# A hybrid decoder step on one core: four instead of three prompt blocks through gathered experts, begun early, with their value rows summed on TensorE

## The chip, the cores and the metric

The kernel runs on one core of a Trainium2 chip. Five engines work beside each other, each with its own queue of instructions that it takes in order: TensorE (PE, matmuls), VectorE (DVE), ScalarE (ACT), GpSimd (POOL), and SyncE (SP), which here only starts transfers. The metric is the time of one execution in microseconds (us).

## The reference, cut to what matters

One layer: a projection, an S5 scan with a GLU beside attention over latent keys, an output mix, and then PEER, a retrieval over 16384 one-neuron experts. 1024 prompt tokens (eight blocks of 128) and 32 tokens of short sequences go through it. The part that the change touches is PEER; per token and head the sixteen best of 128 x 128 key pairs are selected, so 128 experts a token:

```python
s1, i1 = lax.top_k(s[:, :, 0], PEER_TOPK)
s2, i2 = lax.top_k(s[:, :, 1], PEER_TOPK)
top, sel = lax.top_k(cand, PEER_TOPK)                  # of the 16 x 16 sums
idx = jnp.take_along_axis(cidx, sel, axis=-1)
g = jax.nn.softmax(top, axis=-1)
act = jax.nn.gelu(jnp.einsum('qhkd,qd->qhk', jnp.take(u_tab, idx, axis=0), xb))
out = jnp.einsum('qhk,qhkd->qd', g * act, jnp.take(v_tab, idx, axis=0))
```

## The kernel before, in words

The stages follow each other: input projection and S5 tables, the S5 scan, GLU and the queries, keys and values (until about 353 us), attention over the prompt blocks, the output mix (`mix_out`), the scores of the keys (`score`), the selection (`select`), the gates (`Gates`), and the experts. The attention of the short rows over their paged cache (`Sample`) stands later in the text, but the scheduler, which lays the instructions out on a simulated clock and fixes the order of each engine, sets much of it beside the prompt's attention.

PEER is done in two ways. Five blocks (`ND`, 640 tokens) are *dense*: `Gates` turns the selected pairs into a table of gate weights over all 16384 experts, written to DRAM (`g_d`), and `Dense` multiplies the tokens with every expert. It takes four second keys at a time (`group`); per second key it loads and splits 128 rows of each table into two parts of reduced precision (`split`: a cast on ACT, a difference on DVE), makes the first product `da` in two halves of 320 tokens (`mm3`, three matmuls a term), applies GELU on ACT and the gates on DVE, splits again, and after four keys makes the second product, `dres` for two blocks that stay in PSUM and `dy` for three whose sums DVE adds into `yac`.

The other three blocks and the short rows are *sparse* (`peer_sparse`): for each of a token's 128 slots POOL gathers one expert row per partition, a tile of 128 x 1024, by an indirect DMA into a ring of five tiles (`RB`). The first table's tiles `pu` are multiplied with the token and summed by DVE (L1328), the second table's tiles `pv` are weighted and added into `pacc` by DVE (L1336). The gathers and both operations stand in the text behind the dense stage and are set beside it. Selection of the sparse blocks is also beside the dense stage.

`weave` sets one list of steps between another by weights that the steps give out.

Of the kernel before, what the change touches and what calls it, by code (L numbers as in the profile page):

```python
# [20 lines left out]
D = 1024  # L21
# [13 lines left out]
class Small:  # L35
    """Elementwise helpers on small fp32 tiles."""
# [107 lines left out]
def rstd_of(nc, pool, ss, n, cols, inv, name, gain=1.0):  # L144
    """gain / sqrt(ss * inv + eps) for [n, cols], with one Newton step."""
# [11 lines left out]
def rstd_dve(nc, pool, ss, n, cols, inv, name, gain=1.0, bufs=None):  # L157
    """gain / sqrt(ss * inv + eps) for [n, cols]: exponent estimate and three Newton steps."""
# [92 lines left out]
def build(ctx, nc, tc, a):  # L251
# [69 lines left out]
    hold = ctx.enter_context(tc.tile_pool(name="hold", bufs=1))  # L321
    idx = hold.tile([128, NSP, 128], I32, name="idx")
    gws = hold.tile([128, NSP, 128], F32, name="gws")
    idn = hold.tile([128, NS], I32, name="idn")
    gwn = hold.tile([128, NS], F32, name="gwn")
    es = ExitStack()
    with right():
        smp = Sample(es, nc, tc, a, ident, keep, x1_d, xn_d)
    dense, sparse = list(range(ND)), list(range(ND, NB))
    wq_d = dram.tile([16, 128, 2, 8, 128], F32R, name="wq_d")  # L330
    drive(attention(nc, tc, a, ident, qkv, o_d, dense + sparse, lambda pool: split_wq(nc, a, pool, wq_d)))
    drive(mix_out(nc, tc, a, ident, gl_d, o_d, x1_d, xn_d, dense + sparse + [NB]))

    xd = ctx.enter_context(tc.tile_pool(name="xd", bufs=1))
    xt = (xd.tile([128, 8, TD], F32R, name="xdh"), xd.tile([128, 8, TD], F32R, name="xdl"))
    er = ExitStack()
    slots = er.enter_context(tc.tile_pool(name="slots", bufs=1))
    i1T = slots.tile([128, TD], F32, name="i1T")
    i2T = slots.tile([128, TD], BF16, name="i2T")
    wT = slots.tile([128, TD], F32, name="wT")  # L340
# [7 lines left out]
    def take_dense(b, i1, i2, w, pool, pp):  # L348
        tp = pp.tile([128, 3, 128], F32, name=f"slt{b}", tag="slt")
        for j, (src, dst) in enumerate(((i1, i1T), (i2, i2T), (w, wT))):  # L350
            nc.tensor.transpose(tp[:, j], src, ident)
            nc.scalar.copy(dst[:, b * 128 : b * 128 + 128], tp[:, j])

    def take_sparse(b, i1, i2, w, pool, pp):
        ns = 128 if b < NB else NS
        f = pool.tile([128, 128], F32, name=f"fi{b}", tag="cand")[:, :ns]
        nc.vector.scalar_tensor_tensor(f, i1, 128.0, i2, OP.mult, OP.add)
        nc.vector.tensor_copy(idx[:, b - ND] if b < NB else idn, f)
        nc.gpsimd.tensor_copy(gws[:, b - ND] if b < NB else gwn, w)

    with ExitStack() as er2:
        tv, ti = tops(er2, ND, "d")
        drive(score(nc, tc, a, ident, xn_d, dense, lambda b: tv[:, b], lambda b: ti[:, b], "d", wq_d, xt))
        pools = ranks(er2, nc, tc, a, "d")
        for b0, n in DSEL:
            bs = slice(b0, b0 + n)
            select(nc, pools, dense[bs], tv[:, bs], ti[:, bs], take_dense)
    eb = ExitStack()
    gb = Gates(eb, nc, tc, a, i1T, i2T, wT, g_d)

    top_s = []

    def rest():
        yield from smp.run()
        es.close()
        with right():
            top_s.extend(tops(ctx, NSP, "s") + tops(ctx, 1, "n", 2))
        pick = lambda k: lambda b: top_s[k][:, b - ND] if b < NB else top_s[2 + k][:, 0]
        yield from score(nc, tc, a, ident, xn_d, sparse + [NB], pick(0), pick(1), "s", wq_d, None, "right")

    weave(rest(), (x for tb in range(NTB) for x in gb.run(tb)), STEP_US / (TD // GT))
    with right():
        dense_mm = Dense(ctx, nc, tc, a, ident, xt, g_d, x1_d)
    eb.close()
    er.close()
    dense_mm.run()
    with right(), tc.issue_after(gb.last.ins):
        pools = ranks(ctx, nc, tc, a, "s")
        for b0, n in SSEL:
            bs = slice(b0, b0 + n)  # L390
            select(nc, pools, sparse[bs], top_s[0][:, bs], top_s[1][:, bs], take_sparse, 4)
        select(nc, pools, [NB], top_s[2], top_s[3], take_sparse, 4, 2)
    with right():
        ring = ctx.enter_context(tc.tile_pool(name="ring", bufs=1))
    peer_sparse(nc, tc, a, ring, dense_mm.pa, x1_d, xn_d, idx, gws, idn, gwn)
# [7 lines left out]
def weave(steps, others, every):  # L403
# [7 lines left out]
    drive(others)  # L411


STEP_US = 300
GLU_AT = 4
MX = 2
DSEL = ((0, 5),)
# [1371 lines left out]
```

## Time and profile before

| | |
|---|---|
| median of three runs | 3569.2 us (3562.8 to 3575.3) |
| span of the profiled execution | 3563.9 us, of which PE is busy 3220.8, DVE 2750.0, ACT 1254.6, POOL 1259.3 |
| dense stage, about 1580 to 3500 us | PE busy 1816.9, DVE 1611.2, DMA share 0.89 |
| after the dense stage | 64 us |

The profile gives the span from the first to the last instruction; the whole time of that one execution is not given beside it. Busy time of PE counts pipelined matmuls until their modelled ends, so how far PE is from its pace is read from the spacing of the starts. A group's line gives its count, its busy time, the mean of one, and then the idle time of the engine before it.

### The profile page before, as it was taken

The numbers are of one execution on the slowest core, as the hardware profiler recorded it, in microseconds if no ns is written. First come the engines' busy times: TensorE is split into PE (matmuls) and PEld (weight loads), VectorE is DVE, ScalarE is ACT, GpSimd is POOL, SyncE is SP. The second block draws the span as 40 slices with busy tenths as digits, with TensorE's granted clock in tenths as the row PEclk, the third lists the DMA queues.
The fourth block names the chain that finished last, engine by engine and source line by source line (L and its number), as shares of the span: only waits on it lengthen the run. The fifth ranks groups of instructions, "written<-read, shape, count | busy, mean of one in ns | idle before, by whom it ended". The sixth has DMA issues, their size and how long they took to land.

```text
span 3563.9 us, 52091 instructions
## 1 busy us (share of the span) xinstructions
PE 3220.8 (90%) x19216; PEld 2847.0 (80%) x19216; DVE 2750.0 (77%) x5752; ACT 1254.6 (35%) x2355; POOL 1259.3 (35%) x1033
## 2 busy tenths in 40 slices
PE   8899899999997578979889999999999999999993
PEld 7778687777896458968778889888889898888892
DVE  7674554455479988989788989778889897878887
ACT  4333454442322598772222222222222221212220
POOL 1020100000000000006455665556556665655665
PEclk9889799999998799989999999999999999999996
DMA  3334951134331046559788999978899998889998
GB/s 134 83 88 134 311 178 39 35 127 136 142 128 44 25 160 228 204 209 315 272 290 297 317 332 331 341 277 318 304 330 331 338 350 295 311 299 317 329 325 290
DMA packets 337278, 829.82 MB, mean 233 GB/s; under 512 B 35576, under 2 KB 165752, under 8 KB 326208
## 3 DMA queue, kind: packets, MB, share of 16 engines
q0 software_dynamic: 129024, 505.47, 39.5%
q1 hardware_dynamic: 108144, 253.06, 20.4%
q10 hardware_dynamic: 99856, 67.97, 6.6%
q8 instruction: 151, 2.47, 0.3%
q14 instruction: 103, 0.84, 0.1%
HBM read 732.02 MB, written 93.00 MB: 231 GB/s over the span
## 4 chain that ended last, share of the span: by engine, by line
PE 37%; DMA 18%; DVE 15%; issue 15%; POOL 10%; ACT 6%; ACTq 0%; POOLq 0%; SPq 0%; DVEq 0%
POOL pv L1334 7%; DMA pv<-in_peer_v_dram,idx 5%; DMA gt<-g_d 5%; DVE pu L1328 4%; POOL pu L1326 3%; DMA pu<-in_peer_u_dram,idx 3%; PE po L686 2%; PE gps L1215 2%; ACT gbuf L1216 2%; PE s L665 2%; ACT hw L1210 2%; PE kk L139 2%; PE kk L141 1%; PE kk L140 1%; DVE pacc L1336 1%
## 5 line engine op out<-in xcount | busy, mean ns | idle before, releaser
L1326 POOL DMA_INDIRECT pu<-in_peer_u_dram,idx x384 | 537.4, 1399 | 416.1 <-DVE pact L1328 268.8
L139 PE MATMUL da<-xdh,uh 128*128 128x320 f32 x2048 | 639.3, 312 | 31.7 <-ACT ga L1288 30.4
L1334 POOL DMA_INDIRECT pv<-in_peer_v_dram,idx x384 | 541.7, 1411 | 354.7 <-DVE pacc L1336 244.9
L141 PE MATMUL da<-xdh,ul 128*128 128x320 f32 x2048 | 637.1, 311 | 0.8 <-DVE ul L129 0.8
L140 PE MATMUL da<-xdl,uh 128*128 128x320 f32 x2048 | 637.4, 311 | 0.0
L1336 DVE SCALAR_TENSOR_TENSOR pacc<-pv,pw,pacc 128x1024 f32<-128x1024 f32 x416 | 533.3, 1282 | 98.3 <-DMA pv<-in_peer_v_dram,idx 84.5
L1328 DVE CUSTOM_DVE_ANT_0 pu<-pu,pxn 128x1024 f32<-128x1024 f32 x416 | 500.6, 1219 | 80.9 <-DMA pu<-in_peer_u_dram,idx 71.3
L139 PEld LDWEIGHTS da<-xdh,uh 128*128 128x128 f32 x2048 | 390.1, 190 | 43.6 <-ACT ga L1288 33.7
L140 PEld LDWEIGHTS da<-xdl,uh 128*128 128x128 f32 x2048 | 390.1, 190 | 8.2
L141 PEld LDWEIGHTS da<-xdh,ul 128*128 128x128 f32 x2048 | 389.9, 190 | 5.7 <-DVE ul L129 1.3
L139 PE MATMUL dy<-vh,hh 128*128 128x512 f32 x768 | 313.8, 410 | 79.3 <-DVE yac L1303 79.2
L140 PE MATMUL dy<-vl,hh 128*128 128x512 f32 x768 | 309.0, 404 | 0.0
L141 PE MATMUL dy<-vh,hl 128*128 128x512 f32 x768 | 305.2, 405 | 0.0
L128 ACT CAST uh<-ur 128x1024 fp32r<-128x1024 f32 x128 | 134.5, 1051 | 450.4 <-PE da L140 449.9
L1288 ACT ACTIVATE ga<-da 128x320 f32<-128x320 f32 x256 | 110.2, 433 | 430.2 <-PE da L141 408.1
L139 PEld LDWEIGHTS dy<-vh,hh 128*128 128x128 f32 x768 | 151.0, 197 | 117.7 <-DVE yac L1303 87.3
L1215 PE MATMUL gps<-hw,h 128*128 128x128 f32 x1280 | 175.5, 291 | 49.8 <-ACT gbuf L1216 41.8
L1215 PEld LDWEIGHTS gps<-hw,h 128*128 128x128 f32 x1280 | 162.6, 201 | 62.6 <-ACT gbuf L1216 51.7
L128 ACT CAST hh<-ga 128x640 fp32r<-128x640 f32 x128 | 93.1, 727 | 334.9 <-DVE ga L1290 207.3
L139 PE MATMUL dres<-vh,hh 128*128 128x512 f32 x512 | 196.7, 391 | 1.1 <-ACT vh L128 1.1
L140 PE MATMUL dres<-vl,hh 128*128 128x512 f32 x512 | 197.3, 391 | 0.0
L141 PE MATMUL dres<-vh,hl 128*128 128x512 f32 x512 | 187.0, 391 | 1.8 <-DVE hl L129 1.8
(545 smaller groups left out, 7015.7 us busy)
## 6 DMA issues: line engine op xcount, KB each, us to landing
ur<-in_ut_dram SPq DMA_DIRECT2D x128, 512.0 KB, 6.5
vr<-in_peer_v_dram SPq DMA_DIRECT2D x128, 512.0 KB, 6.2
g_d<-gbuf SPq DMA_DIRECT2D x20, 2048.0 KB, 7.3
gt<-g_d ACTq DMA_DIRECT2D x32, 1280.0 KB, 18.3
wq_d<-wq POOLq DMA_DIRECT2D x16, 1024.0 KB, 6.9
rwd<-wq_d POOLq DMA_DIRECT2D x16, 1024.0 KB, 5.2
rws<-wq_d POOLq DMA_DIRECT2D x16, 1024.0 KB, 5.3
wqr<-in_peer_wq_dram SPq DMA_DIRECT2D x16, 512.0 KB
```

What stands on the lines that cost most here:

```text
L128: nc.scalar.copy(hi, raw)
L139: nc.tensor.matmul(out, ah, bh, start=(first and i == 0), stop=False)
L140: nc.tensor.matmul(out, ah, bl, start=False, stop=False)
L141: nc.tensor.matmul(out, al, bh, start=False, stop=(last and i == n - 1))
L665: nc.tensor.matmul(s[:, c0 : c0 + w], qT[:, h, :], kT[:, h, c0 : c0 + w], start=True, stop=c0 + w != nk)
L686: nc.tensor.matmul(po[p0 : p0 + 64, h // 2], va[:, k, h * 64 : (h + 1) * 64], pT[:, k, :], start=(k == 0), stop=(k == b))
L1215: nc.tensor.matmul(ps[:, j, :], h1[:, j0 + j], hw[:, j0 + j], start=True, stop=True)
L1288: nc.scalar.activation(ga[:, cs], ps[:, :HW], AF.Gelu_apprx_tanh)
L1326: nc.gpsimd.indirect_dma_start(out=ur, out_offset=None, in_=a["peer_u"], in_offset=bass.IndirectOffsetOnAxis(ap=ix[:, s : s + 1], axis=0))
L1328: nc.vector.tensor_tensor_reduce(ur, ur, xn, 1.0, 0.0, OP.mult, OP.add, act[:, s : s + 1])
L1334: nc.gpsimd.indirect_dma_start(out=vr, out_offset=None, in_=a["peer_v"], in_offset=bass.IndirectOffsetOnAxis(ap=ix[:, s : s + 1], axis=0))
L1336: nc.vector.scalar_tensor_tensor(acc, vr, w[:, s : s + 1], acc, OP.mult, OP.add)
```

## The change

Four blocks (0 to 3, "early") now go through attention, output mix, scores and selection first and are the sparse ones; blocks 4 to 7 ("late") follow and are dense. The gathers of the early blocks are set between all that follows by an outer `weave` with a pace (`PACE`), from the first selection on. The query weights are split in each `score` instead of once into DRAM. `mix_out` runs three times, in plain fp32. `Gates` makes one small compare-and-scale per token on DVE instead of wider operations on DVE and ACT. The dense first product is one pass of 512 tokens, one block's sum stays in PSUM (`NR`), the gates have two buffers (`GB`) and the ring has seven tiles.

The first table's rows are handled as before. For the second table a tile now holds the 128 selected rows of *one* token, a slot a partition. Four tokens, 32 apart, make a step: their weights are set into column 31 of a zero tile `z`, and per half row four matmuls with a window of 32 columns of it add each token's weighted sum into its own row of its own 32 rows of `acc` in PSUM. The short rows come last.

```diff
+    def rest():
+        yield from attention(nc, tc, a, ident, qkv, o_d, late)
+        sparse.sums(ctx)
+        yield 0.0
+        yield from mix_out(nc, tc, a, gl_d, o_d, x1_d, xn_d, late, "l")
...
+        yield from weave(short(), (x for tb in range(NTB) for x in gb.run(tb)), STEP_US / (TD // GT))
...
+        yield from dense_mm.run()
+
+    drive(weave(rest(), sparse.run(), 1.0 / PACE, True))
...
-STEP_US = 300
+STEP_US = 200
+PACE = 0.75
...
+D0 = 4
+ND = NB - D0
...
-HW = TD // 2
+HW = 512
...
-        w = sp.tile([128, 2, 8, 128], F32R, name=f"rw{tag}_{m}", tag="w", bufs=3)
-        nc.gpsimd.dma_start(w, wq_d[m])
+        w = sp.tile([128, 2, 8, 128], F32R, name=f"rw{tag}_{m}", tag="w")
+        raw = sp.tile([128, 8, 128], F32, name=f"rwr{tag}_{m}", tag="raw")
+        nc.sync.dma_start(raw, a["peer_wq"][m])
         wh, wl = w[:, 0], w[:, 1]
+        split(nc, wh, wl, raw)
...
-                mm3(nc, z[:n], [(ch[:, k, :n], cl[:, k, :n], wh[:, k, hs], wl[:, k, hs]) for k in range(kt)])
+                for k in range(8):
+                    nc.tensor.matmul(z[:n], cat[:, k, :n], w[:, k, hs], start=(k == 0), stop=(k == 7))
...
+            ps = pp.tile([128, 128, GT], F32, name=f"gps{t}", tag="gps")
+            for j in range(GT):
+                c = slice(t + j, t + j + 1)
+                nc.vector.tensor_scalar(hw[:, j], self.iota, i2T[:, c], wT[:, c], OP.is_equal, OP.mult)
+                nc.tensor.matmul(ps[:, :, j], h1[:, j], hw[:, j], start=True, stop=True)
+            nc.scalar.copy(buf[:, :, t0 : t0 + GT], ps)
...
-GT = 8
-GV = 4
+GT = 4
 GI = 4
-UB, VB, RB, GB = 2, 2, 5, 1
-NR = 2
+UB, VB, RB, GB = 2, 2, 7, 2
+NR = 1
...
-            nc.vector.scalar_tensor_tensor(acc, vr, w[:, s : s + 1], acc, OP.mult, OP.add)
...
+        for i in range(m):
+            z = self.z[i % len(self.z)]
+            nc.scalar.copy(z[:, :, 31], wT.rearrange("p (j i) -> p j i", j=4)[:, :, i])
+            rows = [self.row(f"pv{b}_{i}_{j}", "peer_v", ix[:, j * m + i : j * m + i + 1]) for j in range(4)]
+            for h in range(2):
+                for j in range(4):
+                    nc.tensor.matmul(acc[j * 32 : j * 32 + 32, h], z[:, j, 31 - i : 63 - i], rows[j][:, h * 512 : h * 512 + 512],
+                                     start=(i == 0), stop=(i == m - 1))
+            yield 6.0
```

Three places show what the change moves. On PE, in the middle of the dense stage, the order before is the first product `da` of a key and then the second product `dy`:

```order
L139 MATMUL da_320_24377<-xdh,uh_24338 128x320
L140 MATMUL da_320_24377<-xdl,uh_24338 128x320
L141 MATMUL da_320_24377<-xdh,ul_24339 128x320
L139 MATMUL dy_4_0_24306<-vh_23930,hh_23934 128x512
L140 MATMUL dy_4_0_24306<-vl_23931,hh_23934 128x512
L141 MATMUL dy_4_0_24306<-vh_23930,hl_23935 128x512
```

In the new kernel the same place has value matmuls between them; `pacc` is the sum of a block, `pv_19_2` the gathered tile of step 19 and column group 2, `zc` the zero tile with the weights:

```order
L1353 MATMUL pacc_21808<-pv_19_2_24238,zc_4544 32x512
L139 MATMUL da_0_24309<-xdh,uh_24296 128x512
L140 MATMUL da_0_24309<-xdl,uh_24296 128x512
L141 MATMUL da_0_24309<-xdh,ul_24297 128x512
L139 MATMUL da_0_24309<-xdh,uh_24296 128x512
L140 MATMUL da_0_24309<-xdl,uh_24296 128x512
L1353 MATMUL pacc_21808<-pv_19_3_24240,zc_4544 32x512
L1353 MATMUL pacc_21808<-pv_19_0_24234,zc_4544 32x512
L1353 MATMUL pacc_21808<-pv_19_1_24236,zc_4544 32x512
L1353 MATMUL pacc_21808<-pv_19_2_24238,zc_4544 32x512
L1353 MATMUL pacc_21808<-pv_19_3_24240,zc_4544 32x512
L141 MATMUL da_0_24309<-xdh,ul_24297 128x512
```

The eight matmuls of a step, two halves by four column groups, are not kept together: those of the first half stand singly, the last of it with the second half in a run of five.

On POOL, the queue before has the first gather `pu` behind the last cache rows (`cache`, `krc`, `srow` of the short rows' attention) and the last query weights (`rws`):

```order
L802 DMA cache_1_13074<-in_cache_dram,pidx 128x2304
L818 COPY krc_13620<-cache_0_13072 128x256
L818 COPY krc_13620<-cache_1_13074 128x256
L871 MEMSET srow_14120 128x32
L1070 DMA rws_15518<-wq_d 128x2048
L359 COPY gws<-re_28963 128x128
L1326 DMA pu_0_29405<-in_peer_u_dram,idx 128x1024
```

Now it has them between the cache rows:

```order
L870 MEMSET srow_11853 128x32
L801 DMA cache_1_10955<-in_cache_dram,pidx 128x2304
L801 DMA cache_0_11499<-in_cache_dram,pidx 128x2304
L817 COPY krc_11602<-cache_1_10955 128x256
L1308 COPY gws<-re_6439 128x128
L817 COPY krc_12145<-cache_0_11499 128x256
L1315 DMA pu_0_6933<-in_peer_u_dram,idx 128x1024
```

The gathers have moved from behind the selection of every block to behind that of block 0, ahead of most of the short rows' attention.

On DVE, in the gates, the order before is compares `h` and weighted copies `hw` of eight tokens, with the key search `tis` of the sparse blocks between them:

```order
L1179 MAX_INDEX tis<-tvs,rsss_0_15011 128x8 x3
L1180 MATCH_REPLACE rsss_0_15011<-tvs,rsss_0_15011 128x128 x3
L1181 MAX tvs<-rsss_0_15011 128x8 x2
L1206 TENSOR_TENSOR h_440_13740<-giota,i1T 128x1024
L1211 TENSOR_TENSOR hw_13742<-h_440_13741,wT 128x512
```

Now it is four tokens at a time, with the dots of gathered rows (L1330) between them:

```order
L1178 TENSOR_TENSOR h_28_15522<-giota,i1T 128x512
L1182 TENSOR_SCALAR hw_15523<-giota,i2T,wT 128x128 x4
L1178 TENSOR_TENSOR h_32_15537<-giota,i1T 128x512
L1182 TENSOR_SCALAR hw_15538<-giota,i2T,wT 128x128 x4
L1330 ISA pu_124_17564,pact_8995<-pu_124_17564,pxn_8993 128x1024
L1330 ISA pact_8995 128x1
L1330 ISA pu_125_17567,pact_8995<-pu_125_17567,pxn_8993 128x1024
```

So the dots, which all stood in the dense stage, are now in the gates too. In the new order 323 of 544 dots and 384 of 1088 value matmuls stand ahead of the first second-product matmul of the dense stage.

## Rows read from the trace of the kernel before

**Rows 1.** The page, part 1: busy us, share of the span, instructions.

```profile
PE 3220.8 (90%) x19216; PEld 2847.0 (80%) x19216; DVE 2750.0 (77%) x5752; ACT 1254.6 (35%) x2355; POOL 1259.3 (35%) x1033
```

**Rows 2.** Busy time by stage; columns as its first line says.

```profile
core 0: us, PE busy (x) PEld busy (x) DVE busy (x) ACT busy (x) POOL busy (x), PEclk, DMA share, GB/s
...
353.00:765.00 412.00, 397.63 (x2614) 311.67 (x2613) 219.54 (x435) 196.04 (x503) 27.07 (x45) 0.95 0.40 130
765.00:1108.00 343.00, 326.07 (x2116) 294.54 (x2115) 210.27 (x901) 103.34 (x252) 16.39 (x29) 0.97 0.41 140
1108.00:1225.00 117.00, 64.03 (x418) 55.55 (x418) 114.84 (x494) 49.28 (x113) 3.98 (x3) 0.77 0.07 27
1225.00:1580.00 355.00, 288.99 (x1995) 262.50 (x1995) 314.23 (x806) 302.54 (x537) 9.09 (x17) 0.95 0.50 188
1580.00:3500.00 1920.00, 1816.90 (x9912) 1641.69 (x9912) 1611.15 (x2274) 463.46 (x663) 1127.40 (x807) 0.97 0.89 314
3500.00:3564.00 64.00, 10.68 (x28) 6.11 (x28) 46.20 (x43) 0.23 (x1) 34.19 (x29) 0.59 0.77 272
```

**Rows 3.** Timeline of PE in the dense stage: start, us, instruction.

```profile
2050.01 0.31 PE L141 MATMUL da<-xdh,ul 128*128 128x320 f32 x1
2050.15 0.31 PE L139 MATMUL da<-xdh,uh 128*128 128x320 f32 x1
...
2063.75 0.39 PE L139 MATMUL dy<-vh,hh 128*128 128x512 f32 x1
2063.97 0.39 PE L140 MATMUL dy<-vl,hh 128*128 128x512 f32 x1
```

**Rows 4.** Waits of PE, dense stage: us in total, times, longest.

```profile
PE dy L139 <- DVE yac L1303: 75.9, 22, 8.4
```

**Rows 5.** DVE by line: busy us, mean ns, idle before.

```profile
L1336 DVE SCALAR_TENSOR_TENSOR pacc<-pv,pw,pacc 128x1024 f32<-128x1024 f32 x416 | 533.3, 1282 | 98.3 <-DMA pv<-in_peer_v_dram,idx 84.5 <-DMA pv<-in_peer_v_dram,idn 9.6
L1328 DVE CUSTOM_DVE_ANT_0 pu<-pu,pxn 128x1024 f32<-128x1024 f32 x416 | 500.6, 1219 | 80.9 <-DMA pu<-in_peer_u_dram,idx 71.3 <-DMA pu<-in_peer_u_dram,idn 8.8
L129 DVE TENSOR_TENSOR ul<-ur,uh 128x1024 fp32r<-128x1024 f32 x128 | 155.9, 1218 | 2.3 <-ACT uh L128 2.1
...
L1206 DVE TENSOR_TENSOR h<-giota,i1T 128x1024 f32<-128x1024 f32 x80 | 97.4, 1219 | 18.5 <-PE gps L1215 18.3
...
L1211 DVE TENSOR_TENSOR hw<-h,wT 128x512 f32<-128x512 bf16 x80 | 86.1, 1077 | 0.0
L1205 DVE TENSOR_TENSOR h<-gkey,i2T 128x1024 bf16<-128x1024 bf16 x80 | 54.7, 685 | 16.5 <-ACT hw L1210 16.0
...
L161 DVE TENSOR_SCALAR rv_s<-ssq 128x128 f32<-128x128 f32 x7 | 1.5, 219 | 0.1
```

**Rows 6.** Timeline of PE: column-tiled fp32 matmuls, passes counted singly.

```profile
709.54 1.93 PE L912 MATMUL spo<-cache,spT 128*32 128x256 f32 x32
711.40 0.61 PE L913 MATMUL spo<-lns,spN 32*32 32x256 f32 x2
711.95 1.09 PE L686 MATMUL po<-pT,va 128*64 128x128 f32 x8
...
3556.76 3.33 PE L1345 MATMUL psy<-pacc,psel 128*32 128x512 f32 x4 [48.58 <-DVE pacc L1336]
```

**Rows 7.** Timeline of DVE: two dots in a row.

```profile
2321.50 1.22 DVE L1328 CUSTOM_DVE_ANT_0 pu<-pu,pxn 128x1024 f32<-128x1024 f32 x1
...
2322.65 1.22 DVE L1328 CUSTOM_DVE_ANT_0 pu<-pu,pxn 128x1024 f32<-128x1024 f32 x1
```

**Rows 8.** Waits of DVE, from the dense stage to the end.

```profile
DVE ga L1290 <- DMA gt<-g_d: 108.4, 15, 10.4
DVE pacc L1336 <- DMA pv<-in_peer_v_dram,idx: 84.5, 68, 6.0
```

**Rows 9.** DMA issues by line: count, us to landing.

```profile
pu<-in_peer_u_dram,idx POOLq DMA_INDIRECT x384, 7.1
```

**Rows 10.** Timeline of POOL: first and last of the last 32 gathers.

```profile
3493.24 0.94 POOL L1334 DMA_INDIRECT pv<-in_peer_v_dram,idn  x1 [1.77 <-DVE pact L1328]
...
3549.82 1.02 POOL L1334 DMA_INDIRECT pv<-in_peer_v_dram,idn  x1 [0.30 <-issue]
```

More of the change, by code (lines that the diff above doesn't have):

```diff
@@ L320, in build @@
     right = lambda: tc.using_default_side("right")
[L321 to L326, printed above, removed]
-    with right():
[L328 to L340, printed above, removed]
+    late = list(range(D0, NB))
+    with right():
+        ring = ctx.enter_context(tc.tile_pool(name="ring", bufs=1))
+        sparse = Sparse(nc, tc, a, ring, ident, x1_d, xn_d)
+        es = ExitStack()
+        smp = Sample(es, nc, tc, a, ident, keep, o_d)
     def tops(es, n, tag, heads=8):
@@ L361, in build @@
[L361 to L388, printed above, removed]
+    early = list(range(D0))
+    drive(attention(nc, tc, a, ident, qkv, o_d, early))
+    drive(mix_out(nc, tc, a, gl_d, o_d, x1_d, xn_d, early, "e"))
+    with ExitStack() as e1:
+        tv, ti = tops(e1, D0, "e")
+        drive(score(nc, tc, a, ident, xn_d, early, lambda b: tv[:, b], lambda b: ti[:, b], "e", None))
+        pools = ranks(e1, nc, tc, a, "e")
@@ L400, in drive, with weave @@
         pass
-def weave(steps, others, every):
-    due = 0.0
+def weave(steps, others, every, weighed=False):
+    due, cost = 0.0, 1.0
     for w in steps:
         due += w
-        while due >= every:
-            due -= every
-            next(others, None)
-    drive(others)
-STEP_US = 300
+        while due >= every * cost:
+            due -= every * cost
+            got = next(others, None)
+            if got is None:
+                due, cost = 0.0, 1e9
+            elif weighed:
+                cost = got
+        yield w
+    for x in others:
+        yield 0.0
+STEP_US = 200
+PACE = 0.75
 GLU_AT = 4
 MX = 2
-DSEL = ((0, 5),)
-SSEL = ((0, 1), (1, 1), (2, 1))
-NSP = 3
-ND = NB - NSP
+D0 = 4
+ND = NB - D0
+DSEL = ((0, 2), (2, 2))
+SSEL = ((0, 1), (1, 1), (2, 1), (3, 1))
 TD = ND * 128
@@ L626, with attention @@
 QP = 0
-RAWB = 2
 WRB = 4
-def split_wq(nc, a, pool, wq_d):
-    for m in range(16):
-        w = pool.tile([128, 2, 8, 128], F32R, name=f"wq{m}", tag="wq", bufs=2)
-        raw = pool.tile([128, 8, 128], F32, name=f"wqr{m}", tag="wqr", bufs=RAWB)
-        nc.sync.dma_start(raw, a["peer_wq"][:, m * 128 : (m + 1) * 128].rearrange("(k p) n -> p k n", p=128))
-        split(nc, w[:, 0], w[:, 1], raw)
-        nc.gpsimd.dma_start(wq_d[m], w)
-        yield
-def attention(nc, tc, a, ident, qkv, o_d, blocks, job, side="left"):
+def attention(nc, tc, a, ident, qkv, o_d, blocks, side="left"):
     with ExitStack() as e1, ExitStack() as e2:
@@ L724, in start @@
                 pend[i] = scores(b, h, qTs_[b], rss[b])
-        extra = job(sp)
+        for b in range(blocks[0]):
+            keys(b)
         fetch(blocks[0])
@@ new lines, in run @@
+    def run(self):
+        blocks = list(range(D0)) + [NB]
+        yield from self.up(blocks[0])
+        for b, nxt in zip(blocks, blocks[1:] + [None]):
+            ups = self.up(nxt) if nxt is not None else iter(())
+            for c in self.down(b):
+                yield c
+                spent = 0.0
+                while spent < c:
+                    u = next(ups, None)
+                    if u is None:
+                        break
+                    spent += u
+                    yield u
+            yield from ups
```

270 lines of the change are left out of this document (141 added, 129 removed).

## The prediction

> **What bounds the kernel now.** I read the page's first part, then the busy times stage by stage, then TensorE's waits, then the lines, and last the timeline for spacings. TensorE (PE) is busy 90% of the span and VectorE (DVE) 77% [rows 1], but these are averages over stages with different limits, so the reader should go to the stage table [rows 2]. From 1580 to 3500 us the dense experts run: PE is busy 1817 of 1920 us, DVE 1611, the DMA engines 0.89. From 1108 to 1225 us, the selection, DVE is busy 114.8 of 117 us and PE 64. From 1225 to 1580 us, the gates, DVE has 314 and PE 289 of 355 us. The last 64 us are gathers that outlast the dense stage.
>
> Inside the dense stage PE is the limit, and its own pace says so. The matmuls of 320 columns start 0.147 us apart and those of 512 columns 0.228 us apart [rows 3]. 6144 of the first and 3840 of the second make 903 + 876 = 1779 us of the 1920 (93%). The largest wait of PE there is 75.9 us for the accumulator that DVE adds up [rows 4]. DVE is second: it holds 832 gathered tiles there, 416 dots of 1.22 us and 416 weighted adds of 1.28 us [rows 5].
>
> So two budgets have to be counted anew: DVE ahead of the dense stage, and PE inside it. I take each part of the change on the engine that is the limit where it lands. The counts of instructions are from the new program's order, the durations from the rows.
>
> **Dense blocks, five to four.** The first product becomes one pass of 512 columns, 3072 matmuls, and the second 3072 of 512: 6144 x 0.228 = 1400 us. That takes 379 us from PE. On DVE a second key's gating and split go from 640 to 512 elements; both are out of DVE's way there, see below.
>
> **Value rows on PE.** DVE loses 416 x 1.28 = 533 us, all from the dense stage. PE gets 1088 plain fp32 matmuls of 32 output rows and 512 columns, two passes each. Two prices are in the trace. Together: 32 passes of 256 columns on four column groups in turn start at 709.54 and the next kind at 711.40, so 0.058 us each [rows 6]; at 512 columns 0.116 a pass, 0.23 a matmul. Alone: the four passes of 512 columns at the end, all on one column group, take 3.33 us, 0.83 a pass [rows 6]. That stretch had a granted clock of 0.59 [rows 2], mostly the 1.2 GHz level, and at 2.4 GHz I take half, 0.85 a matmul with issue. Entering and leaving the tiled form: the two passes of 256 columns at 711.40 take 0.55 us where two quarters of 0.83 are 0.42, so 0.13.
>
> Which price holds is decided by the order on PE. A step has eight of these matmuls, but the order mostly sets three of them singly between full-width matmuls, and then five in a run. A run costs as many single prices as its busiest column group has members: three singles and a run of five cost 3 + 2 = 5 prices where eight together cost 2. Of the 1088, 704 in 286 runs stand behind the first second-product matmul; they come to 376 single prices. 376 x 0.85 + 286 x 0.13 = 357 us, against 704 x 0.23 = 162 us if all went together. I take 357, since the order on the engine is fixed. So PE in the dense stage has 1400 + 357 = 1757 us of work, against 1779: of the 379 us taken away nearly all comes back.
>
> The Trainium skill, "TensorEngine Tiling (Array Packing)", Tiling Modes, says that a change of tiling mode drains the array. The 0.13 us above is this trace's bound for it, 37 us over the 286 runs; without it the sum would be 1720. The same page's Theoretical Speedup gives up to four times for 32 columns; the trace shows 0.42 / 0.116, or 3.6, where nothing stands between. Were it had by scattered matmuls as well, that is the first rival.
>
> What fills the stage around it: DVE there falls to 221 dots at 1.15 us spacing [rows 7], 254 us, about 128 x 3.5 = 448 for the dense splits and 115 for the accumulators, 817 us or 45%. So half of the present loss of 7% should go (the accumulator wait, and the gate loads that DVE waited 108 us for [rows 8], which get a second buffer). 1757 / 0.965 = 1820 us. Bounds: (1400 + 162) / 0.99 = 1580 and 1757 / 0.92 = 1910. The z copies (136, four elements a row) fall on ScalarE, busy 463 of 1920 us there [rows 2].
>
> **DVE ahead of the dense stage.** Now it is busy 219.5 + 210.3 + 114.8 + 314.2 = 859 us from 353 to 1580 [rows 2]. Added: 323 of the 544 dots stand ahead of the first dense value split, 323 x 1.15 = 371. The selection of three prompt blocks and the short rows, now hidden in the dense stage, at most 115 / 5 = 23 a block, 72 in all. The query weights are split three times instead of once, 2 x 16 x 1.22 = 39. Taken: splits of the output weights and their inputs, 17 x 1.22 = 21. Gates: 97 + 86 + 55 = 238 [rows 5] become 128 compares of 512 elements at 0.69 (a 512-element operation, half of 1.22 and its fixed part) and 512 small ones at 0.22 [rows 5], 201, so 37 less. Sum 859 + 371 + 72 + 39 - 21 - 37 = 1283 us.
>
> Of these, about 260 come before the first gather. That stretch is PE's: attention, output mix and scores of four blocks with the short rows' attention beside them. At the same spacings the order holds 332 us of PE work up to the first selected indices, where the kernel now has 370 in the 412 us from 353 to 765: 332 / 0.90 = 369, so 353 + 369 and a landing of 7.1 us [rows 9] give 730. Then DVE has 1283 - 260 = 1023 us left. Its share where it is the limit is 0.98 in the selection and 0.89 in the gates [rows 2]; I take 0.93: 1100 us, and the dense stage starts at 1830 instead of 1580. Bounds: 0.99 gives 1763, 0.88 gives 1893. PE has about 840 us in that stretch, so it does not set it. The gathers nearly do: 512 of them stand there; the last 32 of today went out in 3549.82 - 3493.24 = 56.6 us, 1.8 each [rows 10], which makes 920 us.
>
> The output mix in plain fp32 and three loads of its weights: 16 matmuls at the single price of 0.85 us are 14 us a block instead of 48 x 0.228 = 11, inside the 332 and 840 and not on DVE, so nothing here. What waits behind a late row: a dot on DVE has the selection and gate instructions queued behind it, a value matmul on PE the dense ones; that is the second rival.
>
> **Sum.** 1830 + 1820 + 10 (last add of 128 x 1024 and its store, in place of today's 64 us) = 3660 us of span. The profiled execution has a span of 3563.9; its own whole time is not given, the median of the runs is 3569.2, 5 us more. So 3665 us, 2.7% slower.
>
> **Rivals.** First, faster: the column groups share the array even where a full-width matmul stands between their parts, so a value matmul costs 0.23 us wherever it is. Then the dense stage is (1400 + 162) / 0.965 = 1620 and the time 1830 + 1620 + 10 + 5 = 3465. It decides below about 0.37 us a matmul in the dense stage: 3569 - 15 - 1830 = 1724, times 0.965 less 1400 is 264 us for 704. For it: the 3.6-fold at 709.54. Against it: a full-width matmul needs every column group, and 191 of the 286 runs are single. By the tiling page's factor of four it would be 704 x 0.85 / 4 = 150 us, 3455 in all.
>
> Second, slower still: PE takes its instructions in order and waits for rows. With seven row buffers the last row of a step can be asked for only when the step before is done; five issues of up to 1.8 us and 7.1 us landing are 16 us, where a step has 1820 / 88 = 21 us of PE work, but only about 10 in the last 31 steps, which have few dots between. With 2 us lost in each of the 88 steps the time is 3665 + 176 = 3840. For it: DVE waits today 84.5 us for value rows with five buffers [rows 8]. Against it: two more buffers and fewer gathers per us (576 in 1820).
>
> Third, no change: the gathers fill every gap of DVE and of PE. 730 + 1023 / 0.99 = 1763, 1757 / 0.985 = 1784, in all 3562. For it: DVE at 0.98 in the selection. Against it: both at once, with one engine's order waiting for the other's.
>
> **How the numbers follow.** The forecast has 0.47, the first rival 0.26, the second 0.17, the third 0.10. About 0.3% is what a measurement of this kernel tells from no change, 3559 to 3580. Slower: 0.47 + 0.17 = 0.64. The third is within it with 0.07 and faster with 0.03, the first faster with 0.25 and within it with 0.01: faster 0.28, same 0.08. The forecast's own range is 3585 to 3760. The range that holds eight in ten reaches into the first rival, 3430, leaving out 0.10 of it and its lower bound of 3360, and to the second's 3840, leaving out 0.08.
>
> **What would show it.** In the profile after: the first dense value matmul near 1830 us, and DVE over 90% busy from 730 to there with PE near 75%. In the dense stage the value matmuls should start about 0.43 us a pass apart when single, with PE over 95% and DVE near 45% busy. A row of single value matmuls that start 0.1 us a pass apart, or a dense stage of 1650 us, would make the forecast wrong by its first step, a dense start near 1650 by its second, and long waits of PE for gathered value rows would show the second rival.

## The result, and the profile after

The changed kernel takes 4115.3 us (median of four runs, 4108.7 to 4118.0), beside 3567.8 us for the kernel before in the same comparison: a ratio of 1.153, 95% interval 1.150 to 1.156. The forecast was 3665 us, range 3430 to 3840. The sign is right and the size is not: 547 us slower, not 96.

The page's first part after the change; it answers to [rows 1]:

```profile
PE 3570.0 (87%) x17177; PEld 2438.7 (59%) x17177; DVE 2389.0 (58%) x6061; ACT 1046.1 (25%) x2005; POOL 1362.2 (33%) x1245
```

PE is busy 349 us longer than in [rows 1] and idle 203 us longer, and DVE has less to do than before. So no engine is full; as with [rows 2], the stages must be read one by one. I cut the span where something begins: 789 the first gather, 1097 the first scores of the late attention, 1343 the first value matmul, 1884 the gates, 2262 the first dense value split (L129, the line below the table), 4072 shortly behind the last `dres` (4068). The last line of the table takes the first five together.

```profile
core 0: us, PE busy (x) PEld busy (x) DVE busy (x) ACT busy (x) POOL busy (x), PEclk, DMA share, GB/s
353.00:789.00 436.00, 394.97 (x2216) 309.67 (x2214) 265.25 (x1023) 161.79 (x404) 16.87 (x27) 0.93 0.32 101
789.00:1097.00 308.00, 115.54 (x702) 96.91 (x701) 260.31 (x733) 57.68 (x146) 196.61 (x156) 0.65 0.82 279
1097.00:1343.00 246.00, 231.49 (x1616) 176.98 (x1614) 111.27 (x206) 101.14 (x259) 4.71 (x9) 0.97 0.13 45
1343.00:1884.00 541.00, 426.71 (x1676) 223.13 (x1675) 364.53 (x1355) 92.88 (x161) 275.50 (x232) 0.82 0.82 291
1884.00:2262.00 378.00, 261.39 (x1301) 167.47 (x1301) 292.26 (x779) 81.25 (x151) 167.90 (x141) 0.78 0.76 287
2262.00:4072.00 1810.00, 1788.18 (x7398) 1175.52 (x7397) 856.52 (x1158) 410.86 (x597) 646.85 (x564) 1.00 0.75 258
4072.00:4116.00 44.00, 33.85 (x132) 13.39 (x130) 4.66 (x6) 0.40 (x2) 13.17 (x15) 0.92 0.70 239
...
353.00:2262.00 1909.00, 1430.10 (x7505) 974.16 (x7503) 1293.62 (x4093) 494.74 (x1118) 661.59 (x564) 0.83 0.61 213
```

```profile
L129 DVE TENSOR_TENSOR vl<-vr,vh x128: 1210/1222/1297, 2262.0 to 4034.4; 128x1024 fp32r<-128x1024 f32 x128
```

The reader is to see three things. From 2262 us on it is as forecast: PE busy 1788 of 1810 us. The DVE work ahead of that is as forecast too: 1294 us, where the sum gave 1283. But it fills only 68% of 1909 us, and PE 75%. The two engines are full in turn: from 789 to 1097 DVE is 85% busy and PE 38%, from 1097 to 1343 PE is 94% busy and DVE 45%. The dense stage starts 432 us later than forecast because of that.

Why they take turns is seen on two queues. First the late attention's own first load, on the queue of SP, and beside it the last operation of the early selection, the cast of the fourth block's indices on DVE (count, then first and last start):

```profile
1070.22 0.29 SPq L654 DMA_DIRECT2D hsel<-in_hsel_dram  x1
```

```profile
L1311 DVE CAST idxT<-slt x4: 280/283/288, 789.5 to 1070.3; 128x128 int32<-128x128 f32 x4
```

Both stand at 1070. The late attention's memory pools are opened in the text behind the closing of the early selection's, and the load starts when that selection ends. The selection in turn shares DVE with the dots, the first of which starts at 793.

Second, the queue of POOL: start, us, instruction, and in brackets the idle time before it with what ended it.

```profile
1041.34 0.94 POOL L1315 DMA_INDIRECT pv<-in_peer_v_dram,idxT  x1 [1.89 <-DVE rv_s L167]
...
1345.97 0.96 POOL L1315 DMA_INDIRECT pv<-in_peer_v_dram,idxT  x1 [100.10 <-PE pacc L1353]
```

Between these two rows POOL has only the short sequences' cache rows, with small copies and fills beside them. The ring holds seven value rows that wait for their matmuls, and the first value matmul starts at 1343, when the late attention has ended (its last scores start at 1310): the accumulators' pool (`vsum`) is opened in the text behind the late attention. For 305 us no row is gathered, and no dot runs.

In the dense stage the prices can be read from PE's timeline, in a stretch where nothing waits:

```profile
2901.73 0.40 PE L140 MATMUL da<-xdl,uh 128*128 128x512 f32 x1
2902.06 1.05 PE L1353 MATMUL pacc<-pv,zc 128*32 128x512 f32 x2
2903.03 0.50 PE L141 MATMUL da<-xdh,ul 128*128 128x512 f32 x1
2903.37 0.40 PE L139 MATMUL da<-xdh,uh 128*128 128x512 f32 x1
...
2904.29 0.39 PE L141 MATMUL dy<-vh,hl 128*128 128x512 f32 x1
2904.61 1.90 PE L1353 MATMUL pacc<-pv,zc 128*32 128x512 f32 x10
2906.44 0.50 PE L139 MATMUL dy<-vh,hh 128*128 128x512 f32 x1
2906.78 0.40 PE L140 MATMUL dy<-vl,hh 128*128 128x512 f32 x1
```

From 2901.73 to 2903.37 there are two dense matmuls at 0.228 and one value matmul of two passes: 1.64 - 0.46 = 1.18 us for a single one. From 2904.29 to 2906.78 there is a run of five: 2.49 - 0.46 = 2.03 us. The difference of 0.85 is one more single price, so a matmul alone costs 0.85 and a run adds 0.33 for going in and out of the tiled form.

### The profile page after: what moved, and what is told of

It is laid out like the page before. It is cut to its first block, busy times and chain, and to the rows that moved or that the text cites. A ratio compares the mean times of both kernels' runs of the same rounds, so it can differ in the third digit from the quotient of the medians.

```text
span 4116.2 us, 48085 instructions
## 1 busy us (share of the span) xinstructions
PE 3570.0 (87%) x17177; PEld 2438.7 (59%) x17177; DVE 2389.0 (58%) x6061; ACT 1046.1 (25%) x2005; POOL 1362.2 (33%) x1245
## 4 chain that ended last, share of the span: by engine, by line
PE 69%; DMA 12%; DVE 7%; issue 7%; POOL 3%; ACT 1%; ACTq 0%; SPq 0%; POOLq 0%; DVEq 0%
PE pacc L1353 11%; PE da L139 5%; PE da L140 5%; PE da L141 5%; DMA pv<-in_peer_v_dram,idxT 5%; PE dy L139 4%; PE dy L141 4%; PE dy L140 4%; DMA pu<-in_peer_u_dram,idx 3%; PE oz L1003 3%; PE gps L1183 3%; DVE pu L1330 2%; POOL pu L1315 2%; PE po L684 2%; PE s L663 2%
## 5 line engine op out<-in xcount | busy, mean ns | idle before, releaser
L1315 POOL DMA_INDIRECT pv<-in_peer_v_dram,idxT x512 | 605.9, 1183 | 828.2 <-PE pacc L1353 641.0
L1330 DVE CUSTOM_DVE_ANT_0 pu<-pu,pxn 128x1024 f32<-128x1024 f32 x544 | 660.2, 1222 | 304.5 <-DMA pu<-in_peer_u_dram,idx 278.3
L1353 PE MATMUL pacc<-pv,zc 128*32 128x512 f32 x2176 | 634.1, 638 | 172.5 <-DMA pv<-in_peer_v_dram,idxT 167.5
L139 PE MATMUL da<-xdh,uh 128*128 128x512 f32 x1024 | 407.4, 398 | 4.0 <-issue 2.5
L141 PE MATMUL da<-xdh,ul 128*128 128x512 f32 x1024 | 406.6, 397 | 3.0 <-DVE ul L129 3.0
L140 PE MATMUL da<-xdl,uh 128*128 128x512 f32 x1024 | 406.9, 397 | 0.0
L139 PE MATMUL dy<-vh,hh 128*128 128x512 f32 x768 | 304.9, 397 | 2.0 <-DVE yac L1271 2.0
L129 DVE TENSOR_TENSOR ul<-ur,uh 128x1024 fp32r<-128x1024 f32 x128 | 156.6, 1224 | 169.5 <-ACT uh L128 138.5
L139 PEld LDWEIGHTS da<-xdh,uh 128*128 128x128 f32 x1024 | 193.1, 189 | 90.3 <-issue 45.1
L141 PEld LDWEIGHTS da<-xdh,ul 128*128 128x128 f32 x1024 | 192.9, 189 | 83.0 <-issue 36.9
L140 PEld LDWEIGHTS da<-xdl,uh 128*128 128x128 f32 x1024 | 193.0, 188 | 81.8 <-issue 44.4
L129 DVE TENSOR_TENSOR vl<-vr,vh 128x1024 fp32r<-128x1024 f32 x128 | 156.2, 1224 | 51.3 <-ACT vh L128 50.5
L139 PEld LDWEIGHTS dy<-vh,hh 128*128 128x128 f32 x768 | 144.5, 188 | 64.1 <-issue 26.0
```

Of the source, the lines that this page charges most:

```text
L139: nc.tensor.matmul(out, ah, bh, start=(first and i == 0), stop=False)
L140: nc.tensor.matmul(out, ah, bl, start=False, stop=False)
L141: nc.tensor.matmul(out, al, bh, start=False, stop=(last and i == n - 1))
L1315: self.nc.gpsimd.indirect_dma_start(out=r, out_offset=None, in_=self.a[table], in_offset=bass.IndirectOffsetOnAxis(ap=ix, axis=0))
L1330: nc.vector.tensor_tensor_reduce(ur, ur, xn, 1.0, 0.0, OP.mult, OP.add, act[:, s : s + 1])
L1353: nc.tensor.matmul(acc[j * 32 : j * 32 + 32, h], z[:, j, 31 - i : 63 - i], rows[j][:, h * 512 : h * 512 + 512], start=(i == 0), stop=(i == ...
```

## The experiments

Where I compare, the start of the dense stage is that of the first `dres` matmul, and its length goes to the start of the last one on L139. First the kernel before (1601 us), then the changed kernel (2288); two numbers at the end of such a line are the first and the last start:

```profile
L139 PE MATMUL dres<-vh,hh x512: 387/389/504, 1601.1 to 3483.1; 128*128 128x512 f32 x171
L139 PE MATMUL dres<-vh,hh x256: 387/389/796, 2288.1 to 4065.7; 128*128 128x512 f32 x128
```

In the diffs "..." stands for what is left out.

**A step's value matmuls together.** The weights are put into `z` by an operation that also reads the step's last row, so that all eight become ready at once; it runs on DVE, where the copy that it replaces ran on ACT.

```diff
-            nc.scalar.copy(z[:, :, 31], wT.rearrange(...)[:, :, i])
             rows = [self.row(...) for j in range(4)]
+            nc.vector.scalar_tensor_tensor(z[:, :, 31], rows[3][:, 0:4], 0.0,
+                                           wT.rearrange(...)[:, :, i], OP.mult, OP.add)
```

> The eight value matmuls of a step become ready at one moment (the weights are put into z by an operation on DVE that also reads the step's last row), so that the order on PE has 140 runs of them in place of 404, 118 of them of eight; in the dense stage 95 runs with 191 single prices in place of 286 with 376. Theory A (scattered matmuls are what is dear: the trace after has 1.18 us for a single between full matmuls, 0.85 of its own and 0.33 for the change of form): 185 x 0.85 + 191 x 0.33 = 220 us less in the dense stage and up to 90 us less ahead of it, 3800 to 3900 us. Theory B (the loss is idle time ahead of the dense stage, from gathers that stand still between 1041 and 1346 us): the dense stage still gains its 220 us, but it starts at 2245 as before, 3890 to 3900. Rival C (PE waits for the rows themselves, and the saved time turns into waiting): 4060 to 4115.

Measured: 3859 us, 256 less (1.081 of before, 1.078 to 1.085). In the timeline of PE a run of eight, 16 passes, stands between dense matmuls:

```profile
2907.43 0.39 PE L140 MATMUL da<-xdl,uh 128*128 128x512 f32 x1
2907.75 1.92 PE L1353 MATMUL pacc<-pv,zc 128*32 128x512 f32 x16
2909.61 0.50 PE L141 MATMUL da<-xdh,ul 128*128 128x512 f32 x1
2909.94 0.39 PE L139 MATMUL da<-xdh,uh 128*128 128x512 f32 x1
```

Its price is 2.51 - 0.46 = 2.05 us, that of a run of five: four groups share the array when they follow each other. The dense stage is 182 us shorter (first to last `dres` 1595, was 1778) and starts 111 us earlier:

```profile
L139 PE MATMUL dres<-vh,hh x256: 387/389/794, 2177.5 to 3772.9; 128*128 128x512 f32 x128
```

So the scattered order is one cause, but half of the loss is left, all of it ahead of the dense stage.

**Two blocks of dots ahead of the first value rows.**

```diff
-        w = self.w[b] = sp.tile([128, 128], F32, name=f"pw{b}", tag="w", bufs=2)[:, :ns]
+        w = self.w[b] = sp.tile([128, 128], F32, name=f"pw{b}", tag="w", bufs=3)[:, :ns]
...
-        yield from self.up(blocks[0])
-        for b, nxt in zip(blocks, blocks[1:] + [None]):
+        for b in blocks[:2]:
+            yield from self.up(b)
+        for b, nxt in zip(blocks, blocks[2:] + [None] * 2):
```

> The dots of blocks 0 and 1 both come ahead of the value rows of block 0. Theory B (POOL's queue stands still from 1041 to 1346 us because value rows fill the ring and their sums cannot begin until the late attention frees their banks): block 1's 128 gathers and dots move into that gap, 150 to 230 us less ahead of the dense stage, 3890 to 3970 us in all, POOL's gap under 100 us. Theory A (price of scattered matmuls alone; the stretch is PE's): the gap fills, but the dense stage starts within 40 us of 2245 and the time is 4070 to 4130.

Measured: 4203 us, 88 more; the dense stage starts at 2400. No theory had that. The block of dots did not move into the gap but for the most part ahead of it; 228 of the first 256 dots start before the late attention's first load, which comes late:

```profile
1201.91 0.29 SPq L654 DMA_DIRECT2D hsel<-in_hsel_dram  x1
```

More dots beside the early selection, 228 in place of 132, made it end 131 us later, and with it the late attention began later. POOL's gap is still there, up to the first value matmul at 1508. That is how theory D came up, that the dots hold up the selection and the selection's memory the late attention.

**Value rows on DVE**, with everything else of the change kept:

```diff
-                    nc.tensor.matmul(acc[j * 32 : j * 32 + 32, h], z[:, j, 31 - i : 63 - i], rows[j][...], ...)
+            vr = self.row(f"pv{b}_{s}", "peer_v", ix[:, s : s + 1])
+            nc.vector.scalar_tensor_tensor(acc, vr, w[:, s : s + 1], acc, OP.mult, OP.add)
```

> Block order, early gathers, dense stage of four blocks and gates as in the changed kernel, but the value rows are weighted and added by DVE as in the kernel before (544 operations of 1.28 us, no value matmul). Theory A or B (value matmuls on PE, by price or by the wait for their banks, are the loss): DVE has 1023 + 697 + 817 us of work from 788 us on, at a share of 0.90 2820, so 3600 to 3700 us. Rival C (the gathers themselves, begun early, hold everything up by transport): 3950 or more.

Measured: 4112 us, the same as the changed kernel. That is not the 3600 to 3700 of theories A and B, and it lies where rival C had it (3950 or more). My sum of 3600 to 3700 made the mistake of the prediction once more: it let DVE work through both stages as if they were one. The windows:

```profile
2000.00:2694.00 694.00, 270.54 (x1047) 232.87 (x1048) 602.67 (x1249) 96.33 (x154) 368.06 (x290) 0.50 0.78 270
2694.00:4094.00 1400.00, 1374.91 (x6035) 1133.61 (x6034) 866.49 (x993) 392.44 (x506) 325.06 (x235) 0.99 0.60 208
```

With value rows on DVE, what stands ahead of the dense stage keeps DVE at 87% from 2000 to 2694, while PE has 39% and the DMA engines 0.78. Then PE is the limit and only 235 of POOL's instructions are left for it to cover. Value matmuls on PE are therefore not the whole cause: the early start costs as much in the other form. Whether DVE or the transport of the rows holds that stretch up, this run alone does not separate.

**The early selection first** (on top of the first experiment): the token rows that block 0's dots read are made to depend on the last early block's indices.

```diff
+    sparse.dep = sparse.idx[:, D0 - 1, 0:1]
...
+        if b == 0:
+            zz = sp.tile([128, 1], F32, name="zz")
+            nc.vector.tensor_scalar(zz, self.dep, 0.0, None, OP.mult)
+            nc.vector.tensor_scalar(xn, xn, zz, None, OP.add)
```

> As e1_together, and the dots of block 0 (all but the gathers of the ring's first seven rows) wait until the selection of all four early blocks is done. Theory D (dots share DVE with the early selection, 788 to 1052 us, and the late attention's loads, at 1070, wait for the memory that the selection gives back): without the 133 dots of 1.23 us the selection ends near 890, the late attention loads near 905 in place of 1070, the first dres of the dense stage comes 165 us earlier than 2177, 3690 us in all. Theory B (the value rows' wait for their banks until the late attention ends): the dots then fill the late attention and the value rows wait less, the same or 30 us more. Rival C (the gathers' transport sets the time ahead of the dense stage, and gathers that begin 100 us later make it start no earlier): 3840 to 3900 us.

Measured: 3780 us, 79 less than e1_together. The late attention's first load and the selection's last cast moved together, as theory D has it:

```profile
881.98 0.29 SPq L656 DMA_DIRECT2D hsel<-in_hsel_dram  x1
```

```profile
L1313 DVE CAST idxT<-slt x4: 278/281/281, 783.2 to 882.1; 128x128 int32<-128x128 f32 x4
```

The load came 190 us earlier (1072 in e1_together). The first value matmul moved too, from 1344 to 1228, with the end of the late attention, as it must if it waits for that attention's banks. The dense stage came only 86 us earlier, at 2091: where the other half went, between the late attention and the gates, I have not separated.

```profile
L139 PE MATMUL dres<-vh,hh x256: 387/389/796, 2091.0 to 3693.8; 128*128 128x512 f32 x128
```

An earlier start of the stage by gathers that begin later is what rival C had excluded, so here transport alone does not set the start.

**Dots from the late scores, and from the gates**: the same dependence on a later tile (the last late block's tokens; its gate weights). The steps of the sparse blocks are also set into the text only from there on, and in the second run the pace is 1.0. The second run's edit, beside that of the first experiment and the `xn` lines of the last one:

```diff
+        sparse.dep = wT[:, TD - 1 : TD]
+        go.append(1)
...
-    drive(weave(rest(), sparse.run(), 1.0 / PACE, True))
+    steps = rest()
+    for _ in steps:
+        if go:
+            break
+    drive(weave(steps, sparse.run(), 1.0 / PACE, True))
...
-PACE = 0.75
+PACE = 1.0
```

> As e1_together, but the dots begin when the tokens of the last late block have been split for the late scores; the scheduler then leaves 29 steps of value rows and the short rows behind the dense stage. Theory D: PE is no more held up ahead of the late scores, dense stage from about 1750 us, 1400 + 72 x 2.04 = 1547 of work at 0.97 is 1595, and a tail of 37 steps x 4 rows x 1.85 = 274 us: 3620 us. Rival C (transport): 1088 gathers at 1.85 from 1300 on end at 3310 and would not be late; if they go slower beside the dense tables, at 2.3 us, 3800.

> As e1_together, but the dots begin only when the late selection is done, with the gates. Theory D: the stages ahead take what they took before the change or a little less, dense stage from 1600 us, 1400 + 86 x 2.04 = 1575 at 0.97 is 1625, tail 40 steps x 4 x 1.85 = 296 us: 3500 to 3520 us, faster than the kernel before. Rival C (transport: 1088 gathers in what is left, at 2.1 us or more): 3900.

Measured: 4048 and 4079 us, both far above what I expected, and above rival C's 3800 and 3900 as well. In e5_from_score the dense stage starts at 2068 (1750 expected), and 388 us follow its last `dres` (274 expected). The windows of e6_from_gates, cut at the gates, the dense stage and its end:

```profile
353.00:1574.00 1221.00, 1021.21 (x5730) 787.90 (x5729) 716.92 (x2821) 403.85 (x931) 38.22 (x60) 0.86 0.28 89
1574.00:2005.00 431.00, 246.04 (x1222) 198.55 (x1223) 404.97 (x990) 79.83 (x135) 269.65 (x208) 0.66 0.90 335
2005.00:3660.00 1655.00, 1586.90 (x7391) 1161.78 (x7389) 991.59 (x1470) 391.94 (x509) 847.65 (x685) 0.99 0.89 319
3660.00:4077.00 417.00, 156.71 (x697) 34.33 (x697) 54.65 (x116) 0.84 (x4) 188.13 (x190) 0.60 0.73 250
```

```profile
L139 PE MATMUL dres<-vh,hh x256: 387/389/796, 2024.3 to 3656.0; 128*128 128x512 f32 x128
```

Two of my terms fail. Without a dot to compute, the gates begin at 1574; in the kernel before all dense blocks are selected by 1225 [rows 2]. So the changed order of the stages is some 350 us longer even without the dots: the scores of all eight blocks and of the short rows and two selections now stand ahead of the gates, and PE is busy 1021 us until there, where it was busy 788 until 1225. Against e4_sel_first the matmuls of the gates begin 178 us earlier, but they take 410 us with 165 dots beside them, not 302 with 65, and the dense stage starts at 2024, only 67 us earlier: most of what is won ahead of the gates is lost in them. And the 40 steps that the order leaves behind the dense stage, with 32 gathers for dots of the short rows between them, take 417 us, not 296. There POOL waits for PE in each step:

```profile
3903.37 0.94 POOL L1323 DMA_INDIRECT pv<-in_peer_v_dram,idxT  x1 [3.70 <-PE pacc L1365]
3904.61 0.94 POOL L1323 DMA_INDIRECT pv<-in_peer_v_dram,idxT  x1 [0.30 <-issue]
...
3907.10 0.94 POOL L1323 DMA_INDIRECT pv<-in_peer_v_dram,idxT  x1 [0.30 <-issue]
3911.74 0.94 POOL L1323 DMA_INDIRECT pv<-in_peer_v_dram,idxT  x1 [3.71 <-PE pacc L1365]
```

Four issues that start 1.24 us apart, the last of 0.94 us, and then 3.7 us for a buffer: with seven buffers a step takes 8.4 us there.

> As e6_from_gates, with the value matmuls scattered as in the changed kernel (339 runs with 499 single prices from the dense stage on, of which the last 31 steps stand behind it). Theory A, prices 0.85 and 0.33 as read in the trace after: in the dense stage about 437 single prices and 337 runs, 483 us in place of 86 x 2.04 = 175: 310 us slower than e6_from_gates, about 3820 us. If the price were only in the waiting for rows, the two would be equal.

Measured: 4242 us, 164 more than e6_from_gates, where 310 were expected. The dense stage starts 45 us later (2069) and takes 1852 us from first to last `dres` in place of 1632, 220 more; the tail behind it is 100 us shorter. A step of the tail takes 6.5 us there in place of 8.4. My reading of that, not shown by a run of its own, is that a single matmul can start when its own row has landed and gives its buffer back at once. Theory A holds with a smaller size.

**Eight row buffers** (on e4_sel_first, with one `z` in place of three to make room, so two edits in one):

```diff
-UB, VB, RB, GB = 2, 2, 7, 2
+UB, VB, RB, GB = 2, 2, 8, 2
...
-        self.z = [pool.tile([128, 4, 63], F32, name=f"zc{k}") for k in range(3)]
+        self.z = [pool.tile([128, 4, 63], F32, name=f"zc{k}") for k in range(1)]
```

> As e4_sel_first, with eight row buffers in place of seven (and one zero tile z in place of three, to make room). Theory E (with seven buffers the last row of a step is asked for only when the step before is done; behind the dense stage of e6_from_gates a step of four rows takes 8.4 us where its four issues take 5.0): PE's waits there and ahead of the dense stage shrink, dense stage 40 to 80 us earlier than 2091, 3690 to 3740 us. Rival: the rows' transport sets the pace, whatever the buffers: 3765 to 3790 as e4_sel_first.

Measured: 3688 us, 92 less. The size is as theory E had it, the place only in part: the dense stage does not start earlier (2102, against 2091 in e4_sel_first), but is 40 us shorter and has a tail of 27 us in place of 85.

```profile
2080.00:3666.00 1586.00, 1577.18 (x7401) 1162.78 (x7400) 857.41 (x1232) 393.90 (x510) 663.55 (x564) 1.00 0.82 294
3666.00:3692.00 26.00, 20.54 (x111) 12.37 (x109) 6.55 (x10) 0.00 (x0) 4.69 (x5) 0.98 0.66 228
```

```profile
L139 PE MATMUL dres<-vh,hh x256: 387/389/792, 2102.2 to 3665.4; 128*128 128x512 f32 x128
```

**Attention and output mix of all blocks first**, then early scores, with a pace of 1.0:

```diff
-    drive(attention(nc, tc, a, ident, qkv, o_d, early))
-    drive(mix_out(nc, tc, a, gl_d, o_d, x1_d, xn_d, early, "e"))
+    drive(attention(nc, tc, a, ident, qkv, o_d, list(range(NB))))
+    drive(mix_out(nc, tc, a, gl_d, o_d, x1_d, xn_d, list(range(NB)), "e"))
...
-        yield from attention(nc, tc, a, ident, qkv, o_d, late)
...
-        yield from mix_out(nc, tc, a, gl_d, o_d, x1_d, xn_d, late, "l")
...
-PACE = 0.75
+PACE = 1.0
```

> The changed kernel with attention and output mix of all eight blocks ahead of the early scores, so that only late scores, selection and gates follow the early selection (pace 1.0 so that no step is left behind the dense stage; value matmuls scattered, 452 single prices and 357 runs from the dense stage on, where the changed kernel has 376 and 286). Theory D (the two passes one behind the other, each through attention, mix, scores and selection, with the late one waiting for the early selection's memory, are what made the dense stage late): first gather near 1110, first dres near 1900 in place of 2288, and 76 x 0.85 + 71 x 0.33 = 88 us more value matmuls in the dense stage: 3810 us. Rival C (the dots and rows that stand ahead of the dense stage set its start): first dres near 2290, 4150 to 4210.

> e9_hoist with the eight value matmuls of a step together and eight row buffers: theories A, D and E at once. First dres near 1850, dense stage (1400 + 194 x 0.85 + 99 x 0.33) / 0.97 = 1647, tail 80: 3577 us, about the kernel before. If the prices don't add (the rows' transport, 768 of them left for the dense stage at 2.3 us, 1766): 3700.

> As e10_hoist_together_ring8, with the dots of block 0 behind the early selection, as in e4_sel_first. Theory D: late scores start 60 to 80 us earlier and so does the dense stage, but 107 steps in place of 96 are left for it: 11 x 2.04 = 22 us more there: 3500 to 3540. Transport as the limit: 3700 or more.

Measured: 4021, 3682 and 3659 us, where theory D had 3810, 3577 and 3500 to 3540. The rivals are not met either, though 3682 is near the 3700 for transport. With the scattered matmuls kept, the order of the passes (with its pace) is worth 164 us of the dense stage's start (2124), less than the 390 I had expected; with the other edits made, 111 us (e8_ring8 2102, e11_hoist_sel_first 1991). In e10_hoist_together_ring8 the dense stage was expected to start near 1850 and to take 1647 us; it starts at 2084 and takes 1577, so again the start is what failed. The first line is of e9_hoist, the second of e11_hoist_sel_first:

```profile
L139 PE MATMUL dres<-vh,hh x256: 387/389/796, 2123.9 to 3987.9; 128*128 128x512 f32 x128
L139 PE MATMUL dres<-vh,hh x256: 387/389/795, 1991.3 to 3574.7; 128*128 128x512 f32 x128
```

The last kernel is 1.025 of before (1.022 to 1.027), the best of these; none beats the kernel before. Its windows from the first gather on:

```profile
1122.00:1655.00 533.00, 316.56 (x1586) 223.80 (x1590) 485.00 (x1823) 114.81 (x188) 285.78 (x224) 0.71 0.75 267
1655.00:1970.00 315.00, 216.86 (x1312) 171.80 (x1304) 294.80 (x803) 77.46 (x131) 172.15 (x144) 0.80 0.91 346
1970.00:3575.00 1605.00, 1599.02 (x7609) 1169.10 (x7610) 950.87 (x1406) 395.47 (x514) 830.60 (x695) 1.00 0.92 334
3575.00:3654.00 79.00, 41.46 (x228) 15.77 (x226) 8.97 (x18) 0.18 (x1) 32.40 (x35) 0.79 0.78 279
```

Here DVE is 92% busy from the first gather to the dense stage, (485 + 295) / 848, which is the regime that the prediction had assumed, and PE is full in the dense stage. So the transport of the rows, the rival, does not set the dense stage; from 1655 to 1970 us, where the DMA engines are at 0.91 beside DVE's 0.94, it cannot be told from DVE as the limit. What is left against before is then a balance: the dense stage starts 390 us later than at 1601 (with dots and two selections in a row ahead of it), and from its first `dres` to the end it takes 1663 us where before took 1963, 300 less.

## Why the prediction was wrong

**The dense stage** came out right: forecast 1820 us, and from the first dense value split at 2262 to the last second product at 4093 it took 1831. That is in part luck, since two errors cancelled: 0.85 us for a single price was as forecast, but a change of form took 0.33 and not 0.13, 57 us over the 286 runs, and PE was 99% busy, not 96.5%. The 0.13 had been read at 711.40 [rows 6], where the matmuls on both sides are tiled too (128*32 and 128*64), not full-width. That the scattered order decides, and not the shared price of 0.23, was shown by putting the matmuls together (182 us of the stage). So the first rival is out. The Trainium skill, "TensorEngine Tiling (Array Packing)", Tiling Modes, says that a change of tiling mode drains the array. The trace fits that with the 0.33 us of a run, though no run shows that a drain is what this time is. The same page of the Trainium skill gives up to four times for 32 columns, under Theoretical Speedup. A run of eight shows 8 x 0.85 against 2.05 - 0.33 = 1.72 us, close to four, and nothing of it when the members stand apart.

**The failed step** is this one: "Then DVE has 1283 - 260 = 1023 us left. Its share where it is the limit is 0.98 in the selection and 0.89 in the gates [rows 2]; I take 0.93: 1100 us, and the dense stage starts at 1830 instead of 1580." The work was sized rightly: in the four windows from 789 to 2262 us DVE is busy 1028 us. But they last 1473 us, a share of 0.70, which I had bounded at 0.88 to 0.99. That DVE would be the limit all the way was taken from two stages where it was, and carried over to a stretch with two passes, each with a stage of PE's (attention, mix, scores) and one of DVE's (selection). The condition that I gave for it failed too: "PE has about 840 us in that stretch, so it does not set it." In the same windows PE is busy 1035 us, 246 of them with value matmuls, at a granted clock of 0.80 where the dense stage has 1.00. Two engines with as much to do, which are full in turn, take longer than either alone. What I should have asked can be read in the new program: which memory a stage must wait for before its first load, and whether the work that is to fill its gaps can run there at all.

The experiments take the 432 us apart in this way, edit upon edit. The scattered matmuls, whose waits and prices also hold up the gates: 111 us of the dense stage's start. Dots that share DVE with the early selection, by which the late attention starts late: 86. The eighth buffer and the single `z`: 11 in the wrong direction. The order of the passes, late attention behind early selection, with the pace: 111 with the other edits made, 164 alone. Together 297, from 2288 to 1991. The rest, about 135 us, I have not separated, and its cause stays open; the first gather, at 789 and not at 730, came 59 us late. That the seven value rows blocked the ring from 1041 to 1346 is seen in the trace, but the edit meant to lift it made the selection later instead, so its own price stays open too.

**The second rival**, PE waiting for rows, is there, in another place. After the change it is 167.5 us, the largest wait of PE:

```profile
PE pacc L1353 <- DMA pv<-in_peer_v_dram,idxT: 167.5, 51, 10.9
```

Nearly all of it lies between 1700 and 2300 us, ahead of the dense stage and not in it. The ring of seven does cost time in and behind the dense stage, 92 us with the eighth buffer and the single `z`. **The third rival** named what did happen, one engine's order waiting for the other's, as the reason against itself, and I did not make a case of it.

## What to carry to other kernels

A sum of work divided by a share of the limiting engine holds only in a stretch where that engine is the limit throughout; before using it over several stages, list what each stage's first load waits for (memory that the stage before gives back counts) and whether the filler may run in each. Work that is begun early on an engine which a later stage's start depends on can delay that start by its whole length: here 132 dots held the late attention's load up by 190 us, and 86 of that reached the dense stage. Matmuls that were to share the array by column groups had to become ready at one moment here, or the scheduler set some apart, and each of those cost the full price.

## What was not expected of the hardware

A run of value matmuls between full-width matmuls costs 0.33 us beside its members, where 0.13 had been taken. That a run of five and one of eight cost the same, 2.03 and 2.05 us, is as the prediction counts them, by the busiest column group, which has two members in both. And in the tail of e6_from_gates four gathered rows of 512 KB took 8.4 us, 2.1 us a row, at a DMA share of 0.73, with POOL waiting for a buffer in each step: there the ring set the pace.
